# The up projection of a hybrid layer in scaled fp16 halves in place of fp32r halves

## The chip, the cores and the metric

The kernel runs on one core of one Trainium2 chip, as one launch. The metric is the device time of one execution in microseconds (us). A core has five engines that run side by side, each with a queue of its own that is worked off in order: TensorE (PE, matrix products, with its weight loads shown apart as PEld), VectorE (DVE), ScalarE (ACT), GpSimd (POOL) and SyncE (SP, which here only issues DMA transfers). They wait for one another through semaphores.

## What is computed

One layer over 1024 latent tokens of 1024 features. The change lies in the second half, the convolutional feed-forward block. Cut to what matters:

```python
def conv_ffn(h, w_up, conv_w, conv_b, w_down):
    u = h @ w_up                                  # 1024 x 1024 by 1024 x 5632
    up = jnp.pad(u, ((0, 0), (r, r), (0, 0)))     # r = 1
    acc = conv_b
    for j in range(CONV_W):                       # CONV_W = 3
        acc = acc + up[:, j:j + L] * conv_w[j]
    a, g = jnp.split(acc, 2, axis=-1)
    return (jax.nn.silu(g) * a) @ w_down
...
x = x_mid + g2 * conv_ffn(modulate(rms_norm(x_mid, norm2_w[l]), sh2, sc2), w_up[l], ...)
```

So each token is normalised, scaled and shifted channel by channel (the modulation), multiplied by the up weights, mixed with its two neighbours in every channel, gated and multiplied by the down weights.

## The kernel before, in words

**Stages.** Projections and attention come first, then the mLSTM branch, then the tail: the two branch projections and the output projection (up to about 1218 us in the profile), the up projection with convolution and gate, and the down projection (from about 1641 us). The last two share `stage_ffn` (line 2132 on); the preparation stands at the end of `stage_tail`.

**Halves.** All large products are done to nearly fp32 accuracy from two halves of each operand: `split_from` (line 50) writes `hi`, a rounded copy, on ACT (line 47, in `copy_act`), and `lo = src - hi` on DVE (line 54, or line 56, a `scalar_tensor_tensor`, where a scale is given). A product is then three matmuls, hi x hi, hi x lo and lo x hi (`product`, lines 2015 to 2017; `mm3`, lines 163 to 165). Two kinds of halves are in use. In the first stages they are fp16, with a scale from a bound on the size of the data, so that nothing overflows (`ScaledWeights`, line 90 on: ACT squares with a sum along the row, a matmul against a block of ones that adds over partitions, a power -0.5 on POOL). In the tail they are fp32r, without a scale, and each half takes as much memory as the fp32 source.

**Units.** The up projection is done in 22 units `j` of 128 columns of the first and 128 columns of the second half of the up weights. Each unit is one Strassen-like step (2 x 2 x 2 in seven products): from the weight blocks a11, a12, a21, a22 four sums s1 to s4 are made on DVE (lines 2076, 2077, 2085, 2086), and from the activations the seven operands b11, b21, t1, t2, t3, t4, b22 are made once and kept as halves for all units (`put`). In a product the halves of the weights are what PE loads, as 128x128 blocks, and the halves of the activations stream past them, 128x512 at a time; it runs over four row blocks, so it is 4 x 3 matmuls, and a unit is 84. The class `Units` holds the steps of a unit:

- `lead(j)`: the DMA of the unit's weights, 1 MB, on SP (line 2043; two buffers, pool `ffr`), and the split `r1` of a11 and a12. For unit 2 `lead_first` (line 2050) loads the half megabyte for `r1` by itself into another buffer, and `lead(2)` later the whole.
- `first_mm(j)`: products with b11 and b21. `first_ev(j)`: ACT copies bank `pa` to `ua`, DVE adds bank `pc` (line 2065).
- `prep(j)`, `prep2(j)`: the sums s1 to s4, and the splits `q1` (of s1, s2), `q2` (of s3, s4) and `r2` (of a22). `prep_apart` and `prep2_apart` do the same for unit 0 with other buffers.
- `rest(j)`: the other five products, with copies on ACT and adds on DVE (lines 2124, 2126) that empty PSUM between them.

The splits are 128x1024 values (`r1`, `q1`, `q2`) and 128x512 (`r2`); their halves lie in pools `ffo` (`op4`, ten buffers) and `ffq` (`op2`, four buffers), a buffer for each half.

After the unit's products `conv_gate` (line 2145 on) makes the three-tap convolution: ACT multiplies by the middle coefficient and adds the bias (line 2153), two `scalar_tensor_tensor` on DVE add the neighbours (2154, 2155), for both halves of the unit; ACT applies Silu to one (2158), DVE multiplies (2159), SP stores the result to `f_d` (2160). The coefficients come straight from the table `vecT`. Beside this, `sums` prepares the operands of the down projection: beside units 4 to 11 sums of down weights, later sums of the finished hidden rows (four 128x512 steps on DVE a unit, with loads and stores on SP).

**What sets the order.** The loop over `j` at the end (from line 2228 on) states the order in the source: `first_mm(j)`, `first_ev(j)`, `rest(j)`, `lead(j + 1)`, `prep(j + 1)`, `prep2(j + 1)`, `sums(j - 1)`, `conv_gate(j)`. In this part nothing is pinned by hand. The library under the kernel gives out buffers and fills each engine's queue when the program is built, from the source's order as a priority and from what is ready by then, so steps of the next unit stand in the queues among steps of this one. Once the queues are filled, each is worked off strictly.

**The start.** Before unit 0 the residual rows come out of the output projection; each block of 128 tokens gets its factor of the norm (`square`, `scale`), is transposed on PE, and leaves PSUM through `affine` (line 1878), which multiplies by `m2[:, 1]` and adds `m2[:, 0]`, the modulation. `norm_factors` computes `m2[:, 1]` once, long before.

Of the kernel before, what the change touches and what calls it, by code (L numbers as in the profile page):

```python
# [1590 lines left out]
def stage_tail(E, st):  # L1591
# [52 lines left out]

    g1b = tp1.tile([P, D], F32, name="g1b")
# [178 lines left out]
    def norm_factors():  # L1824

        nc.vector.scalar_tensor_tensor(m2[:, 1], m2[:, 1], 1.0, vecT[:, V_N2 : V_N2 + KT], op0=ALU.add, op1=ALU.mult)
        nc.vector.tensor_scalar(m2[:, 1], m2[:, 1], float(D) ** 0.5, None, op0=ALU.mult)

# [9 lines left out]
    xj = tp1.tile([P, 640], F32, name="xj")[:, :512]  # L1838
# [86 lines left out]
    def weight_sums(k, a0, a1, b0, b1, eng=None):  # L1925
# [11 lines left out]
        nc, lambda j: A["w_up"][j], lambda n: rawp.tile([P, KT, 256], F32, tag="raw", name=n), op4, op2,  # L1937
# [32 lines left out]
    scale(4)  # L1970
    U.lead(0)
    U.prep_apart(0, lambda n, dt=F32R: x512(n, dt, 1))
# [23 lines left out]
    U.lead_first(2)  # L1996
# [23 lines left out]
class Units:  # L2020
# [3 lines left out]
    def __init__(self, nc, src, raw, op4, op2, bank, out, B):  # L2024
        self.nc, self.src, self.raw, self.op4, self.op2, self.bank, self.out, self.B = nc, src, raw, op4, op2, bank, out, B
        self.raws, self.R1, self.mid, self.S, self.Q = {}, {}, {}, {}, {}
# [8 lines left out]

    def pair(self, j, nm, new, src):
        p = self.v(new(f"{nm}h{j}")), self.v(new(f"{nm}l{j}"))
        split_from(self.nc, *p, src)
        return [(p[0][:, k], p[1][:, k]) for k in range(p[0].shape[1])]

    def lead(self, j):
        self.raws[j] = raw = self.raw(f"ur{j}")
        self.nc.sync.dma_start(raw, self.src(j))
        if j != 2:
            self.R1[j] = self.pair(j, "r1", self.op4, raw[:, :, 0:P])

    def lead_first(self, j):

        raw = self.v(self.op4(f"uf{j}", F32))
        self.nc.sync.dma_start(raw, self.src(j)[:, :, 0:P])  # L2050
        self.R1[j] = self.pair(j, "r1", self.op4, raw)
# [20 lines left out]
    def prep(self, j):  # L2072
# [6 lines left out]
        self.Q[j] = [self.pair(j, "q1", self.op4, s12)]  # L2079

    def prep2(self, j):
# [5 lines left out]
        self.Q[j] += [self.pair(j, "q2", self.op4, s34), self.pair(j, "r2", self.op2, a22)]  # L2087

    def prep_apart(self, j, new):
# [3 lines left out]
        s1, s2, s3, s4 = [self.v(new(f"s{i}_{j}", F32)) for i in range(1, 5)]  # L2093
# [4 lines left out]
        self.Q[j] = [sum([self.pair(j, f"q1{i}", new, s) for i, s in enumerate((s1, s2))], [])]  # L2098
# [338 lines left out]
```

## Time and profile before

| what | value |
| --- | --- |
| time, median of 3 runs | 1852.91 us (1849.13 to 1855.06) |
| the profiled execution's own time | 1858.65 us |
| its span from first to last instruction | 1856.9 us |
| mean granted TensorE clock | 0.987 of full speed |
| up projection on PE, first to last product | 1218.75 to 1641.6 us |
| 128x512 matmuls in it | 1848 |

A row of a timeline is: start in us, duration in us, engine, line of the code, operation, `output<-inputs` by the names of the tiles, shapes and types, number of instructions, and in square brackets how long the engine had been idle before it and which instruction on which engine ended that wait. `f32` stands there for fp32r operands of matmuls, too. A row of a group ends in the total busy time and the mean duration in ns of one instruction. Matmuls overlap: the row's duration is that of one matmul from its start to its modelled end, so their rate is read from the steps between starts.

### The profile page before, as it was taken

Reading aid. Unit: us, or ns where it says so; the run is one execution under the profiler, and the core shown is the slowest. Engines: PE = TensorE matmul, PEld = TensorE weight load, DVE = VectorE, ACT = ScalarE, POOL = GpSimd, SP = SyncE. Lnnn points to the kernel's source line nnn. Section 1 sums busy time; section 2 is a strip of 40 time slices with the busy share of each in tenths; the row PEclk is TensorE's granted clock in tenths of the full one; section 3 lists DMA queues with packets and bytes.
Section 4 is the critical chain, followed back from the end, with each engine's and each line's share of the span. In section 5 each row is a group of like instructions: output and inputs, shape, how many; then the busy total and the mean of one; then the engine's idle time right before and its main releaser. Section 6 shows DMA issues by size and latency. Waiting matters only on the chain.

```text
span 1856.9 us, 27874 instructions
## 1 busy us (share of the span) xinstructions
PE 1795.2 (97%) x9207; PEld 1286.0 (69%) x9207; DVE 1418.6 (76%) x2864; ACT 1070.7 (58%) x2229; POOL 510.5 (27%) x747
## 2 busy tenths in 40 slices
PE   7889999999998899989999999999999999999999
PEld 3855555555555565656668887878888888888887
DVE  3848878888788685858687787698988998896665
ACT  4747777878787564646356563375444444464441
POOL 2467769687762630303020021000000000000000
PEclk9899999999999899999999999999999999999999
DMA  8647988888787724260449936413454544599751
GB/s 336 234 138 147 195 174 177 190 179 196 148 181 138 217 94 161 79 210 32 148 160 359 362 101 221 168 57 125 159 211 180 186 172 154 197 321 369 262 171 68
DMA packets 302193, 342.47 MB, mean 184 GB/s; under 512 B 176208, under 2 KB 200672, under 8 KB 299232
## 3 DMA queue, kind: packets, MB, share of 16 engines
q1 hardware_dynamic: 287648, 314.47, 56.1%
q10 hardware_dynamic: 14400, 26.22, 4.3%
q8 instruction: 72, 1.18, 0.3%
q14 instruction: 73, 0.60, 0.1%
HBM read 224.61 MB, written 76.16 MB: 162 GB/s over the span
## 4 chain that ended last, share of the span: by engine, by line
PE 77%; DVE 7%; DMA 5%; ACT 5%; issue 4%; POOL 3%; ACTq 0%; SPq 0%; POOLq 0%; DVEq 0%
PE g L706 8%; PE pq L706 6%; PE pa L2015 4%; PE pa L2017 4%; PE pa L2016 4%; PE po L706 3%; PE dx L2015 2%; PE dx L2017 2%; PE dx L2016 2%; PE pb L2017 2%; PE pb L2016 2%; PE pb L2015 2%; PE yb L2015 2%; PE yb L2016 2%; PE yb L2017 2%
## 5 line engine op out<-in xcount | busy, mean ns | idle before, releaser
L850 DVE CUSTOM_DVE_ANT_0 s<-s,maskA,nsink 128x640 f32<-128x640 f32 (+1 forms) x128 | 117.5, 918 | 75.0 <-PE s L845 74.6
L866 DVE TENSOR_TENSOR P<-s,P 128x640 f16<-128x640 f32 (+1 forms) x128 | 100.7, 787 | 1.0 <-ACT s L861 1.0
L860 ACT ACTIVATE P<-s,st 128x640 f16<-128x640 f32 (+1 forms) x128 | 98.3, 768 | 4.2
L706 PE MATMUL g<-hH,fh 128*128 128x512 f16 x256 | 97.9, 382 | 0.0
L706 PE MATMUL g<-hH,fl 128*128 128x512 f16 x256 | 97.8, 382 | 0.0
L706 PE MATMUL g<-hL,fh 128*128 128x512 f16 x256 | 97.7, 382 | 0.0
L861 ACT ACTIVATE s<-s,st 128x640 f32<-128x640 f32 (+1 forms) x128 | 93.9, 734 | 0.0
L706 PEld LDWEIGHTS <-hH 128*128 128x128 f16 x640 | 62.1, 98 | 36.5 <-DVE t L770 0.4
L858 ACT ACTIVATE st<-st,shift 128x1 f32<-128x1 f32 x128 | 37.6, 294 | 85.4 <-DVE st L850 84.7
L706 PE MATMUL pq<-wha,hH 128*128 128x384 f16 (+1 forms) x256 | 83.9, 328 | 0.1
L706 PE MATMUL pq<-wha,hL 128*128 128x384 f16 (+1 forms) x256 | 83.9, 328 | 0.0
L706 PE MATMUL pq<-wla,hH 128*128 128x384 f16 (+1 forms) x256 | 83.9, 328 | 0.0
L706 PEld LDWEIGHTS <-fh 128*128 128x128 f16 x512 | 48.1, 99 | 47.9 <-issue 1.6
L2153 ACT ACTIVATE cv<-ua,vecT 128x1024 f32<-128x1024 f32 x22 | 27.4, 1246 | 83.9 <-DVE ua L2126 83.9
L1424 POOL TENSOR_SCALAR kwh<-k,gcall 128x128 fp32r<-128x128 f32 x72 | 33.1, 463 | 154.4 <-PE dC L164 57.1
L163 PE MATMUL kv<-whkv,hH 128*128 128x384 f16 x192 | 63.3, 330 | 6.0 <-DVE VL L56 6.0
L2015 PE MATMUL dx<-dwh,dfh 128*128 128x512 f32 (+1 forms) x176 | 68.3, 388 | 0.0
L2017 PE MATMUL dx<-dwh,dfl 128*128 128x512 f32 (+1 forms) x176 | 68.2, 388 | 0.0
L2016 PE MATMUL dx<-dwl,dfh 128*128 128x512 f32 (+1 forms) x176 | 68.2, 387 | 0.0
L47 ACT ACTIVATE dfh<-drf 128x512 fp32r<-128x512 f32 x55 | 34.3, 628 | 58.5 <-PE dx L2016 26.0
L54 DVE TENSOR_TENSOR dfl<-drf,dfh 128x512 fp32r<-128x512 f32 x55 | 37.7, 691 | 36.5 <-ACT dfh L47 36.4
L164 PE MATMUL kv<-wlkv,hH 128*128 128x384 f16 x192 | 63.2, 329 | 0.4
(691 smaller groups left out, 6253.8 us busy)
## 6 DMA issues: line engine op xcount, KB each, us to landing
ur<-in_w_up SPq DMA_DIRECT2D x22, 1024.0 KB
wmb<-in_w_modB SPq DMA_DIRECT2D x48, 256.0 KB
f_d<-cv SPq DMA_DIRECT2D x22, 512.0 KB
wm<-in_w_modA SPq DMA_DIRECT2D x16, 512.0 KB
fr<-in_w_g SPq DMA_DIRECT2D x32, 256.0 KB
drf<-fs_d SPq DMA_DIRECT2D x15, 512.0 KB
drw<-wt_d SPq DMA_DIRECT2D x14, 512.0 KB
w1b<-in_w_cx SPq DMA_DIRECT2D x16, 388.0 KB
```

The lines of the kernel that those rows point to most:

```text
L54: rest = nc.vector.tensor_tensor(lo, src, whole, op=ALU.subtract)
L163: nc.tensor.matmul(ps, lh[:, ls], rh[:, rs], start=start and i == 0, stop=False)
L164: nc.tensor.matmul(ps, lh[:, ls], rl[:, rs], start=False, stop=False)
L706: nc.tensor.matmul(self.ps, x, w, start=self.i == 0, stop=self.i == self.n - 1)
L850: nc.vector.tensor_tensor_reduce(e, e, self.mask, scale=self.ss[:, h : h + 1], scalar=nsink[:, hh : hh + 1], op0=ALU.add, op1=ALU.min, acc ...
L858: nc.scalar.activation(m, st4[:, 8 + h : 9 + h], AF.Identity, bias=shift)
L860: nc.scalar.activation(two[:, :W], e, AF.Exp, bias=m, scale=-1.0)
L861: nc.scalar.activation(e, e, AF.Exp, bias=m, scale=-1.0, accum_out=st4[:, 4 + h : 5 + h])
L866: nc.vector.tensor_tensor(two[:, W : 2 * W], self.e[h], two[:, :W], op=ALU.subtract)
L2015: nc.tensor.matmul(ps, lh, rh, start=start and i == 0, stop=False, skip_group_check=True)
L2016: nc.tensor.matmul(ps, lh, rl, start=False, stop=False, skip_group_check=True)
L2017: nc.tensor.matmul(ps, ll, rh, start=False, stop=stop and i == n - 1, skip_group_check=True)
```

## The change

The up projection goes over to fp16 halves. Its activations are made smaller by one scale, its weights by one scale per unit, both from bounds, and the product of the two is taken off again in the coefficients of the convolution.

- `norm_factors` gets a tail: from the modulation `m2` it bounds the size of the activations (squares with sums on ACT, one matmul against the ones, a chain of tiny steps on POOL and DVE), keeps the scale and its reciprocal in `xs_` (a new 128x2 tile), and multiplies `m2` by the scale.
- `measure(j, raw)` is new, once a unit: two squares with row sums over the whole 128x2048 of raw weights on ACT, two matmuls against the ones that add up into one bank, a step on DVE that reads it, a power -0.5 on POOL (the unit's scale, `f[:, 3:4]`), its reciprocal on DVE, and on POOL the six coefficients of the convolution times both reciprocals.
- All splits of weights get the scale, so `lo` is made by line 56's form (three operands) instead of line 54's; both halves are fp16 and lie in one buffer of the same size that one fp32r half took (`pair16`, `xpair`, `pair4`, `pair2`). The splits of activations stay without a scale, with fp16 results.
- `lead` is cut in three: `fetch` (the DMA), `sizes` (`measure`) and `lead` (the split `r1`). `lead_first` goes. In the loop `fetch(j + 2)` stands ahead of `sums`, `sizes(j + 2)` after `conv_gate(j)`, and `lead(j + 1)` where it was. Before the loop, units 0 and 1 are fetched and measured ahead of their splits, and unit 2 is fetched where `lead_first` stood.
- `conv_gate` takes its coefficients from the unit's `f`.

```diff
     def norm_factors():
         nc.vector.scalar_tensor_tensor(m2[:, 1], ...)
         nc.vector.tensor_scalar(m2[:, 1], m2[:, 1], float(D) ** 0.5, None, op0=ALU.mult)
+        q = tp1.tile([P, 24], F32, name="xbound")
+        nc.gpsimd.tensor_tensor(q[:, 8:16], m2[:, 1], m2[:, 1], op=ALU.mult)
+        nc.scalar.activation(q[:, 16:24], q[:, 8:16], AF.Square, accum_out=q[:, 0:1])
+        nc.scalar.activation(q[:, 16:24], m2[:, 0], AF.Square, accum_out=q[:, 1:2])
+        pb = tp_tile("xbound")
+        nc.tensor.matmul(pb[:, 0:2], E.ones, q[:, 0:2], start=True, stop=True)
+        nc.vector.tensor_scalar(q[:, 2:4], pb[:, 0:2], 1.0, 1e-30, op0=ALU.mult, op1=ALU.add)
+        nc.gpsimd.tensor_tensor(q[:, 4:5], q[:, 2:3], expo[:, 0:1], op=ALU.pow)
...
+        nc.gpsimd.tensor_tensor(xs_[:, 0:1], q[:, 4:5], expo[:, 0:1], op=ALU.pow)
+        nc.vector.reciprocal(xs_[:, 1:2], xs_[:, 0:1])
+        nc.gpsimd.tensor_scalar(m2, m2, xs_[:, 0:1], None, op0=ALU.mult)
+
+    def measure(j, raw):
+        f = tp1.tile([P, 16], F32, tag="uf", name=f"uf{j}", bufs=4)
+        junk = xj16.rearrange("p (k c) -> p k c", k=4)
+        for i in range(2):
+            nc.scalar.activation(junk, raw[:, 4 * i : 4 * i + 4], AF.Square, accum_out=f[:, i : i + 1])
+        pb = tp_tile(f"ub{j}")
+        for i in range(2):
+            nc.tensor.matmul(pb[:, 0:1], E.ones, f[:, i : i + 1], start=i == 0, stop=i == 1)
+        nc.vector.tensor_scalar(f[:, 2:3], pb[:, 0:1], 2.0 ** -26, 1e-36, op0=ALU.mult, op1=ALU.add)
+        nc.gpsimd.tensor_tensor(f[:, 3:4], f[:, 2:3], expo[:, 0:1], op=ALU.pow)
+        nc.vector.reciprocal(f[:, 4:5], f[:, 3:4])
+        nc.gpsimd.tensor_scalar(f[:, 5:6], f[:, 4:5], xs_[:, 1:2], None, op0=ALU.mult)
+        cw = vecT[:, V_CW : V_CW + 132].rearrange("p (i u c) -> p i u c", i=3, u=2)[:, :, :, j]
+        nc.gpsimd.tensor_scalar(f[:, 6:12].rearrange("p (i u) -> p i u", i=3), cw, f[:, 5:6], None, op0=ALU.mult)
+        return f
...
     def put(m, k, src, s=slice(0, 512)):
         if B.setdefault(m, [None] * H)[k] is None:
-            B[m][k] = [x512(f"{m}{x}{k}", pool=homes[m]) for x in "hl"]
+            B[m][k] = xpair(f"{m}{k}", homes[m])
...
     scale(4)
+    U.fetch(0)
+    U.fetch(1)
+    U.sizes(0)
     U.lead(0)
-    U.prep_apart(0, lambda n, dt=F32R: x512(n, dt, 1))
+    U.sizes(1)
+    U.prep_apart(0, lambda n: x512(n, F32, 1), lambda n: xpair(n, 1))
...
     U.prep2_apart(0)
-    U.lead_first(2)
+    U.fetch(2)
...
             put("b22", k, RAW[g][k][:, cols[1]], cols[g])
+    U.sizes(2)
+    U.lead(2)
...
     def pair(self, j, nm, new, src):
-        p = self.v(new(f"{nm}h{j}")), self.v(new(f"{nm}l{j}"))
-        split_from(self.nc, *p, src)
+        p = [self.v(t) for t in new(f"{nm}{j}")]
+        split_from(self.nc, *p, src, scale=self.scale(j))
...
-    def lead(self, j):
+    def fetch(self, j):
         self.raws[j] = raw = self.raw(f"ur{j}")
         self.nc.sync.dma_start(raw, self.src(j))
-        if j != 2:
-            self.R1[j] = self.pair(j, "r1", self.op4, raw[:, :, 0:P])
-
-    def lead_first(self, j):
-
-        raw = self.v(self.op4(f"uf{j}", F32))
-        self.nc.sync.dma_start(raw, self.src(j)[:, :, 0:P])
-        self.R1[j] = self.pair(j, "r1", self.op4, raw)
+
+    def sizes(self, j):
+        self.F[j] = self.measure(j, self.raws[j])
+
+    def lead(self, j):
+        self.R1[j] = self.pair(j, "r1", self.pair4, self.raws[j][:, :, 0:P])
...
             def cw(i):
-                return vecT[:, V_CW + 44 * i + ch : V_CW + 44 * i + ch + 1]
+                o = 6 + 2 * i + (ch >= NFC)
+                return U.F[j][:, o : o + 1]
...
         if 1 <= j < NFC - 1:
-            U.lead(j + 1)
+            if j > 1:
+                U.lead(j + 1)
             U.prep(j + 1)
             U.prep2(j + 1)
...
+        if 1 <= j + 2 < NFC and j:
+            U.fetch(j + 2)
         sums(j - 1, a)
         a = conv_gate(j, *u)
+        if 1 <= j < NFC - 2:
+            U.sizes(j + 2)
```

More of the change, by code (lines that the diff above doesn't have):

```diff
@@ L2020, with __init__ @@
 class Units:
[L2024 to L2026 removed]
+    def __init__(self, nc, src, raw, op4, pair4, pair2, measure, bank, out, B):
+        self.nc, self.src, self.raw, self.op4, self.pair4, self.pair2, self.bank, self.out, self.B = nc, src, raw, op4, pair4, pair2, bank, out, B
+        self.measure = measure
+        self.raws, self.F, self.R1, self.mid, self.S, self.Q = {}, {}, {}, {}, {}, {}
     @staticmethod
```

36 lines of the change are left out of this document (26 added, 10 removed).

## The prediction

> **What bounds the kernel now.** I read the page's busy shares first, then the table of busy time by window over the up projection, then the timeline of each engine through one of its units, and last the timelines around its start.
>
> ```profile
> span 1856.9 us, 27874 instructions
> PE 1795.2 (97%) x9207; PEld 1286.0 (69%) x9207; DVE 1418.6 (76%) x2864; ACT 1070.7 (58%) x2229; POOL 510.5 (27%) x747
> 1400.00:1500.00 100.00, 100.00 (x443) 82.58 (x442) 89.54 (x107) 47.23 (x58) 0.00 (x0) 1.00 0.49 179
> ```
>
> The columns of the last row are the stretch and its length, then PE, PEld, DVE, ACT and POOL busy, the granted clock, DMA. In the middle of the up projection PE never idles, at full clock; DVE is busy 90%, ACT 47%, POOL not at all, the DMA engines half. So PE sets the pace here and DVE is second, not far behind. A busy PE may still issue slowly, so I took the step from one matmul's start to the next.
>
> ```profile
> 1300.18 0.39 PE L2015 MATMUL pa<-b11h,r1h 128*128 128x512 f32 x1
> ...
> 1312.42 0.39 PE L2015 MATMUL pb<-b22h,q2h 128*128 128x512 f32 x1
> ...
> 671.03 0.38 PE L163 MATMUL mo<-hH,wha 128*128 128x512 f16 x1
> ...
> 679.24 0.38 PE L165 MATMUL mo<-hH,wla 128*128 128x512 f16 x1
> ```
>
> The first pair spans 54 steps of the up projection without a gap: 12.24/54 = 0.2267 us. The second spans 38 steps of an earlier stage that already multiplies fp16 halves, same 128x512 shape, full clock: 8.21/38 = 0.2161 us. The change turns the first kind into the second.
>
> **Part by part. PE.** A unit issues 7 products x 4 row blocks x 3 = 84 matmuls, 22 units 1848. 1848 x (0.2267 - 0.2161) = 19.6 us less. This is a saving only where PE stays the last to be ready.
>
> The Trainium skill, "TensorE: Matmul & The Clock Gate", section "Wait — 56ns, not 53.3ns?", gives the warm step as N/2.4 + 2.5 ns, 215.7 ns at N = 512, with no term for the operands' type. The fp16 rows agree (216.1), the fp32r rows do not (226.7). By the rule this term would be nothing, and the whole change some 7 us slower; rival 3 is that case, from rows.
>
> Each `measure` puts two tiny fp32 matmuls against the block of ones into PE's queue. The nearest rows are such pairs:
>
> ```profile
> 680.10 0.28 PE L119 MATMUL wtw_ml<-wqw_ml,ones 128*128 128x4 f32 x2
> 680.24 0.36 PE L119 MATMUL wtw_mlqo<-wqw_mlqo,ones 128*128 128x4 f32 x2
> 680.46 1.74 PE L1520 MATMUL mt<-ident,hf 128*128 128x128 f32 x12
> ```
>
> One pair takes 0.14, the next 0.22 us of queue; 0.18 x 22 = 4.0 us (3.1 to 4.8), if what they multiply is there.
>
> **DVE.** Three splits of 1024 columns and one of 512 per unit become scalar_tensor_tensor; two 128x1 instructions come in.
>
> ```profile
> 1302.17 1.28 DVE L2154 SCALAR_TENSOR_TENSOR cv<-ug,vecT,cv 128x1023 f32<-128x1023 f32 x1
> 1303.37 0.69 DVE L2077 TENSOR_TENSOR s<-s,ur 128x512 f32<-128x512 f32 x1
> ...
> 1306.90 1.22 DVE L2159 TENSOR_TENSOR cv<-cv,cv 128x1024 f32<-128x1024 f32 x1
> 1308.03 0.69 DVE L2085 TENSOR_TENSOR s<-ur 128x512 f32<-128x512 f32 x1
> ...
> 1310.51 1.23 DVE L54 TENSOR_TENSOR q2l<-s,q2h 128x1024 fp32r<-128x1024 f32 x1 [0.59 <-ACT q2h L47]
> 1311.94 1.23 DVE L54 TENSOR_TENSOR r1l<-ur,r1h 128x1024 fp32r<-128x1024 f32 x1 [0.20 <-ACT r1h L47]
> ...
> 1315.12 0.69 DVE L2076 TENSOR_TENSOR s<-ur 128x512 f32<-128x512 f32 x1 [1.35 <-PE pb L2016]
> 1315.73 0.68 DVE L2126 TENSOR_TENSOR ua<-pb,ua 128x512 f32<-128x512 f32 x1
> ...
> 1334.77 0.69 DVE L2126 TENSOR_TENSOR ua<-pb,ua 128x512 f32<-128x512 f32 x1
> 1198.55 0.21 DVE L1861 TENSOR_SCALAR rrx<-rrx 128x1 f32<-128x1 f32 x1 [1.17 <-ACT xj L1858]
> L56 DVE SCALAR_TENSOR_TENSOR wlkv<-wrw_ml,wfw_ml,whkv 128x768 f16<-128x768 f32 x12 | 11.6, 1010 | 0.0
> ```
>
> Back to back the three-operand form occupies DVE 1.20 us (1302.17 to 1303.37), the two-operand form 1.13. The last row shows that an fp16 result costs nothing extra: 1.01 us at 768 columns fits 1.28 at 1023. So 4 x 0.07 = 0.28, and 2 x 0.12 for the tiny ones (a row of 0.21 whose tail overlaps the next): 0.5 us per unit. One unit is 1334.77 - 1315.73 = 19.04 us, which is 84 x 0.2267: PE's own time. In it DVE idles 0.59 and 0.20 for ACT and 1.35 for a buffer that PE still reads; the work is 19.04 - 2.14 = 16.9. The new work is 17.4, and with the two waits for ACT 18.2. PE's new unit is 84 x 0.2161 + 0.18 = 18.3. The wait for PE's buffer is slack: a pair now fits one buffer where it took two, so DVE can run further ahead. PE therefore stays the bound, by 0.1 us. That is thin, and I charge 2 us over 19 steady units for stalls that slip through (0 to the whole gain; rival 1).
>
> **ACT.** Two squares of 1024 columns with their sums per unit, and four splits with a scale from memory.
>
> ```profile
> 4.84 0.22 ACT L369 ACTIVATE sil<-vecT 128x16 f32<-128x16 f32 x1 [2.84 <-DVE vecT L367]
> 10.65 1.06 ACT L392 ACTIVATE xj<-x 128x1024 bf16<-128x1024 f32 x1 [5.60 <-DMA x<-in_ctx]
> 11.62 0.19 ACT L392 ACTIVATION_READ_ACCUMULATOR xj<-x 128x1 f32 x1
> L47 ACT ACTIVATE whkv<-wrw_ml,wfw_ml 128x768 f16<-128x768 f32 x12 | 10.5, 925 | 2.1 <-POOL wfw_ml L122 2.1
> L112 ACT ACTIVATE wjw_ml<-wrw_ml 128x768 bf16<-128x768 f32 x12 | 10.1, 842 | 9.9 <-DMA s_ba<-in_w_ba 7.2 <-DMA wrw_ml<-in_w_ml 2.1 <-ACT VH L47 0.5
> ```
>
> 2 x 1.25 for the squares; a scale from memory adds 0.08 (925 against 842 at one width), four times 0.3: 2.8 us on some 9.0 (47% of 19.04), so 12 of 18.3. The first three rows follow one another in ACT's timeline: no table is loaded between a Silu and a Square, so none is added. It costs nothing while the squares fall into ACT's waits, 4.54 and 3.11 us in one unit; with that cover gone, up to 2.8 us a unit stand before a copy that PE waits for:
>
> ```profile
> 1316.45 1.25 ACT L2153 ACTIVATE cv<-ua,vecT 128x1024 f32<-128x1024 f32 x1 [4.54 <-DVE ua L2126]
> ...
> 1318.54 0.58 ACT L47 ACTIVATE ug<-pa 128x512 f32<-128x512 f32 x1
> ...
> 1324.49 1.06 ACT L2158 ACTIVATE cv<-cv 128x1024 f32<-128x1024 f32 x1 [3.11 <-DVE cv L2155]
> ```
>
> **The added waits.** A split now waits for squares, pair, DVE, POOL's power. Behind it on ACT stand the copies that empty PSUM, for which PE waits. There are two weight buffers, so a unit's weights leave when those of two units before are read, more than a unit (18 us) ahead of their first product; the chain (2.5 + 0.2 + 0.1 + 0.6 us, the power from the row below) fits in that.
>
> ```profile
> L1862 POOL TENSOR_TENSOR rrx<-rrx,expo x8: 548/552/2466, 1180.5 to 1221.9; 128x1 f32<-128x1 f32 x8
> ```
>
> The one of 2466 ns ran while DVE was dense; even two such fit. On SP the transfer moves ahead of a unit's store of `f_d` and the loads for the next stage's sums; its buffer sets when it leaves, so passing them moves nothing, and if it did leave earlier, these 0.5 and 1 MB would come later to places that have a whole unit of time. The bound's own chain depends on `m2`, ready long before the first use, and is priced at nothing; if its cover failed, its two powers and some six tiny steps are 3 to 6 us once.
>
> **The start.** Here a step moves: unit 2 had an early half megabyte of its own; now it waits for a whole weight buffer and the chain.
>
> ```profile
> 1170.19 3.36 SPq L2043 DMA_DIRECT2D ur<-in_w_up  x2
> 1176.42 1.06 ACT L47 ACTIVATE r1h<-ur 128x1024 fp32r<-128x1024 f32 x1 [1.09 <-DMA ur<-in_w_up]
> 1220.80 0.61 SPq L2050 DMA_DIRECT2D uf<-in_w_up  x1
> 1222.40 1.23 DVE L54 TENSOR_TENSOR r1l<-ur,r1h 128x1024 fp32r<-128x1024 f32 x1
> 1238.24 0.50 PE L2015 MATMUL pa<-b11h,r1h 128*128 128x512 f32 x1 [0.22 <-ACT r1h L47]
> 1241.04 0.69 DVE L54 TENSOR_TENSOR r2l<-ur,r2h 128x512 fp32r<-128x512 f32 x1
> 1241.80 11.22 SPq L2043 DMA_DIRECT2D ur<-in_w_up  x2
> 1247.88 0.39 PE L2017 MATMUL pa<-t4h,r2l 128*128 128x512 f32 x1
> 1250.18 1.23 DVE L54 TENSOR_TENSOR q1l<-s,q1h 128x1024 fp32r<-128x1024 f32 x1
> 1252.18 0.39 PE L2015 MATMUL pa<-t2h,q1h 128*128 128x512 f32 x1
> ```
>
> Both first transfers already leave together (1170.19, two issues), so hoisting them moves nothing on SP. Unit 2's can leave when unit 0's weights are read (1241.80, right after the split at 1241.04), lands 6.2 us later (1170.19 to 1176.42) at 1248, and after chain and split serves PE at about 1253. Before, unit 2's first products filled PE in places from 1238.24 and up to 1252.18; now nothing fills there until unit 1's q1 (about 1250.2). PE's last product of unit 0 starts at 1247.88, or up to 1.4 us earlier without the six matmuls of unit 2 among them, so it idles 2.1 to 3.5 us; DVE, spared 1.1 us of unit 2's split there, may give some back. I take 2.7; the ends are 0 and 8 (unit 1 late as well). And 132 matmuls before this point (24 each in the first products of three units, 60 in the rest of one) are paced by DVE's splits of the activations, so 132 x 0.0106 = 1.4 us of the saving is not had. The half megabyte that goes frees nothing that anyone waited for.
>
> Sum: -19.6 + 4.0 + 2.0 + 2.7 + 1.4 = -9.5 us. The profiled execution took 1858.65 us, 1.75 beyond its span, and the median is 5.7 lower; 1858.65 - 9.5 = 1849.2 there, 1843.4 against the median. I say 1843.
>
> **Rivals.** 1: DVE takes over. At 17.4 of 18.3 us it has no room: if its waits for ACT grow from 0.8 to 1.4 us, a unit is 18.8 and the gain 0.24 x 20 units = 4.8 less 2.7 at the start: 1851; at 1.6 us a unit is 19.0: 1855. For it: a load of 95% in a queue that takes nothing out of turn. Against: the freed buffers, which let it work ahead.
>
> 1a, its worse end: POOL, idle until now, shuts DVE out. Three POOL steps a unit, none over the 0.55 us of the power, add at most 1.65 us: 17.4 + 0.8 + 1.65 = 19.85 a unit, 0.81 x 20 + 2.7 = 18.9 us slower, 1872. The trace shows POOL as the loser: beside the power of 2466 ns that began at 1221.9, DVE's split of 1222.40 took its usual 1.23 us. The Trainium skill, "SBUF — State Buffer", section "SBUF: two separate sides", has it that a DVE instruction with two SBUF inputs and a POOL instruction that reads SBUF exclude each other for their whole length, whoever comes first. By that rule DVE can lose too; of the two, this trace bears out only the loss on POOL's side.
>
> 2, slower: PE stalls at a pair. The pair stands in PE's queue ahead of the next unit's matmuls. If its squares were queued behind the last unit's Silu, as the source has it (1324.49 + 1.06 + 2.5 = 1328), PE, done with that unit at 1318.5 (the copy of its last bank starts at 1318.54), would wait 9.5 us. One such wait eats the gain, so it decides from there; two make 1843.4 + 19 = 1862. For it: a queue in order, and a chain over DMA, ACT, PE, DVE and POOL. Against: the queues here follow readiness and not the source. Line 2077 at 1303.37 prepares the unit after the one that PE is at, between two conv steps of the unit before it.
>
> 3: no shorter step, because 0.2267 comes from where these operands lie and not from their type: 4.0 + 2.7 = 6.7 us slower, 1860. Against it stand 38 steps in a row.
>
> **Numbers.** About 0.3% (5.6 us) is what a measurement tells from no change: 1847.3 to 1858.5. The forecast gets 0.55, with a range of its own of 1836 to 1848: the tight steady stage and the start may cost nothing (-4.7) or some 5 us more. Rival 1 gets 0.26, of which 0.05 is still faster and the rest within the bound; 1a 0.03, rival 2 0.11, rival 3 0.05, all slower. Faster 0.60, same 0.21, slower 0.19. The range 1836 to 1859 holds the forecast and rival 1 and leaves out the slower ones.
>
> **What would show it.** Step of 0.216 us between the up projection's matmuls; weight loads f16; unit to unit 18.3 to 18.5; DVE over 93% in mid-stage; squares inside ACT's waits; a PE gap of some 3 us before unit 1's q1. Wrong if units stay near 19 (rival 1), if PE idles before the pair on the ones (2), or if the step keeps 0.2267 (3).

## The result, and the profile after

The changed kernel takes 1882.92 us (median, 1880.09 to 1886.9) against 1853.99 for the kernel before on the same chip: ratio 1.016, 95% interval 1.0129 to 1.019. It is slower by 28.9 us, where 9.5 us less had been forecast.

Page and windows of the changed kernel, and then the second of these windows in the kernel before; the columns of the windows are those of the prediction's row.

```profile
span 1879.9 us, 28210 instructions
PE 1787.9 (95%) x9297; PEld 1130.3 (60%) x9297; DVE 1434.9 (76%) x2910; ACT 1124.2 (60%) x2321; POOL 571.9 (30%) x820
```

```profile
1400.00:1500.00 100.00, 94.32 (x437) 43.29 (x436) 87.26 (x111) 57.94 (x75) 11.50 (x16) 0.98 0.51 179
1500.00:1600.00 100.00, 97.79 (x463) 45.29 (x461) 92.01 (x116) 58.62 (x78) 15.98 (x15) 1.00 0.44 158
```

```profile
1500.00:1600.00 100.00, 100.00 (x443) 82.81 (x442) 86.68 (x103) 47.66 (x58) 0.00 (x0) 1.00 0.47 171
```

PE, which was busy 100 of 100 us in mid-stage, now idles, and DVE is hardly fuller than before (89.6% over the two windows, 88.1% before): nobody is saturated. PE's timeline through a unit shows that the step came out as forecast:

```profile
1574.47 0.38 PE L2066 MATMUL pa<-t,q 128*128 128x512 f16 x1 [0.44 <-ACT ua L47]
...
1582.02 0.38 PE L2068 MATMUL pa<-t,q 128*128 128x512 f16 x1
...
1587.48 0.50 PE L1863 MATMUL ub<-uf,ones 128*128 128x1 f32 x4
1587.84 0.38 PE L2066 MATMUL pa<-b,r 128*128 128x512 f16 x1
...
1593.62 0.38 PE L2066 MATMUL pa<-t,q 128*128 128x512 f16 x1 [0.44 <-ACT ua L47]
```

The first two rows are 35 steps apart: 7.55/35 = 0.2157 us, against 0.2267 before. The pair on the ones takes 0.36 us of the queue. Yet from 1574.47 to 1593.62 a unit still lasts 19.15 us, and this unit and the next begin their second group of products with a wait for ACT.

**Where the 28.9 us are.** Three marks cut the end of the kernel into parts: the last of eight `og` instructions in the output projection (ahead of all that changed but the small steps that bound the activations), the first product with `r2` in unit 0, and that in unit 21. Last `og`, before and then after (the last time in the row's range is the start of the last one):

```profile
L1846 DVE TENSOR_TENSOR og<-op,g1b x8: 683/685/692, 1134.9 to 1173.1; 128x512 f32<-128x512 f32 x8
```

```profile
L1891 DVE TENSOR_TENSOR og<-op,g1b x8: 682/684/692, 1129.1 to 1167.2; 128x512 f32<-128x512 f32 x8
```

First `r2` products of units 0 and 21, before and then after:

```profile
1244.93 0.39 PE L2015 MATMUL pa<-t4h,r2h 128*128 128x512 f32 x1
...
1638.90 0.39 PE L2015 MATMUL pa<-t4h,r2h 128*128 128x512 f32 x1
```

```profile
1255.65 0.38 PE L2066 MATMUL pa<-t,r 128*128 128x512 f16 x1
...
1661.64 0.38 PE L2066 MATMUL pa<-t,r 128*128 128x512 f16 x1
```

The *start* (from `og` to unit 0's `r2`) grew from 71.8 to 88.5 us, 16.6 more; the *units* (to unit 21's `r2`) from 394.0 to 406.0, 12.0 more; the rest to the end from 218.0 to 218.3 us. The sum is 28.9, the difference of the medians; the spans differ by less because the stages ahead ended 5.9 us earlier in the execution profiled after. All runs below are read by these two stretches.

**The start.** PE's, ACT's and SP's rows from the changed kernel's timeline:

```profile
1232.31 0.38 PE L2068 MATMUL pa<-t,q 128*128 128x512 f16 x1
...
1236.00 1.65 ACT L47 ACTIVATE t<-acc 128x512 f16<-128x512 f32 x3
1237.56 0.57 ACT L47 ACTIVATE ua<-pa 128x512 f32<-128x512 f32 x1
1238.19 0.58 PE L2066 MATMUL pa<-t,q 128*128 128x512 f16 x1 [5.50 <-ACT ua L47]
1238.57 0.63 PE L2067 MATMUL pa<-t,q 128*128 128x512 f16 x1
...
1239.95 0.33 SPq L2098 DMA_DIRECT2D ur<-in_w_up  x1
...
1241.98 0.61 PE L2066 MATMUL pa<-t,q 128*128 128x512 f16 x1
...
1244.94 1.06 ACT L1860 ACTIVATE xj<-ur 128x1024 bf16<-128x1024 f32 x1 [5.25 <-DMA ur<-in_w_up]
1246.14 0.59 PE L1863 MATMUL ub<-uf,ones 128*128 128x1 f32 x2 [3.12 <-ACT xj L1860]
```

Two things are to be seen. PE waits 5.50 us for a copy out of PSUM that stands in ACT's queue behind splits of activations (the row of 1236.00 and others ahead of it). Then unit 2's weights leave at 1239.95; ACT, with the squares next in its queue, stands still 5.25 us until they land, and PE, with the pair next in its queue, 3.12 us. After the long wait eight steps last (1241.98 - 1238.57)/8 = 0.426 us, twice the usual.

**Mid-stage.** SP's, ACT's and PE's rows between two units:

```profile
1285.55 0.33 SPq L2098 DMA_DIRECT2D ur<-in_w_up  x1
...
1293.20 1.06 ACT L1860 ACTIVATE xj<-ur 128x1024 bf16<-128x1024 f32 x1 [3.64 <-DMA ur<-in_w_up]
...
1298.04 0.58 ACT L47 ACTIVATE ua<-pa 128x512 f32<-128x512 f32 x1
...
1298.67 0.38 PE L2066 MATMUL pa<-t,q 128*128 128x512 f16 x1 [2.83 <-ACT ua L47]
```

ACT waits 3.64 us for the unit's weights before the first of its two squares; the copy `ua<-pa` comes after that square (the second square stands behind the copy), and PE waits for that copy. Nothing needs the squares yet: the pair that reads them comes in PE's queue at 1311.62. The waits from 1213 to 1665 us, of PE and then of ACT (total, times, longest):

```profile
PE pa L2066 <- ACT ua L47: 19.2, 17, 5.5
PE ub L1863 <- ACT xj L1860: 3.1, 1, 3.1
...
PE pa L2068 <- DVE r L56: 2.8, 1, 2.8
```

```profile
ACT cv L2207 <- DVE ua L2179: 54.6, 16, 5.6
ACT xj L1860 <- DMA ur<-in_w_up: 27.7, 12, 5.3
...
ACT r L47 <- POOL uf L1865: 13.2, 11, 3.5
```

So the theories: **A**, the measuring loses it, since its squares stand on ACT ahead of copies (A1: because they wait for the load; A2: by where they stand). **B**, DVE holds ACT up as soon as a unit is shorter than 19 us (B1 by its order, B2 by its amount of work). **C**, the splits wait for the chain over DVE and POOL.

### The profile page after: what moved, and what is told of

Its sections match the earlier page's. It is cut to its first block, busy times and chain, and to the rows that moved or that the text cites. A ratio compares the mean times of both kernels' runs of the same rounds, so it can differ in the third digit from the quotient of the medians.

```text
span 1879.9 us, 28210 instructions
## 1 busy us (share of the span) xinstructions
PE 1787.9 (95%) x9297; PEld 1130.3 (60%) x9297; DVE 1434.9 (76%) x2910; ACT 1124.2 (60%) x2321; POOL 571.9 (30%) x820
## 4 chain that ended last, share of the span: by engine, by line
PE 52%; DVE 20%; DMA 10%; ACT 8%; issue 5%; POOL 4%; SPq 1%; ACTq 0%; DVEq 0%; POOLq 0%
PE g L706 8%; PE pq L706 5%; PE po L706 3%; DMA ur<-in_w_up 2%; PE dx L2066 2%; PE dx L2068 2%; PE dx L2067 2%; DVE cv L2208 2%; PE dy L2066 2%; PE dy L2068 2%; PE dy L2067 2%; DVE cv L2209 2%; DVE r L56 1%; PE mo L163 1%; PE mo L164 1%
## 5 line engine op out<-in xcount | busy, mean ns | idle before, releaser
L1865 POOL TENSOR_TENSOR uf<-uf,expo 128x1 f32<-128x1 f32 x22 | 26.5, 1204 | 350.8 <-DVE uf L1864 238.2
L2066 PE MATMUL pa<-t,q 128*128 128x512 f16 x176 | 68.1, 387 | 19.2 <-ACT ua L47 19.2
L47 ACT ACTIVATE q<-s,uf 128x1024 f16<-128x1024 f32 (+1 forms) x46 | 50.7, 1106 | 41.7 <-DVE s L2139 21.0
L2067 PEld LDWEIGHTS <-q 128*128 128x128 f16 x352 | 34.7, 99 | 66.8 <-issue 29.2
```

Source lines behind the costliest of these rows:

```text
L47: return nc.scalar.activation(out, in_, AF.Copy, scale=scale)
L2066: nc.tensor.matmul(ps, lh, rh, start=start and i == 0, stop=False, skip_group_check=True)
L2067: nc.tensor.matmul(ps, lh, rl, start=False, stop=False, skip_group_check=True)
```

## The experiments

Each run's median is set against the kernel before on the same chip. "Sum" adds the changes of the two stretches against before; it agrees with the measured difference within 3.4 us, except in row 13 (5.2 us).

| run | start, us | units 0 to 21, us | sum | median | ratio, 95% interval |
| --- | --- | --- | --- | --- | --- |
| before | 71.8 | 394.0 | 0 | 1853.99 | 1 |
| after | 88.5 | 406.0 | +28.7 | 1882.92 | 1.0129 to 1.019 |
| 1 no measuring | 72.1 | 394.2 | +0.5 | 1854.59 | 0.9994 to 1.0023 |
| 2 squares of resident data | 79.6 | 406.7 | +20.5 | 1873.26 | 1.0091 to 1.0147 |
| 3 result not used | 80.6 | 400.3 | +15.1 | 1869.21 | 1.0062 to 1.0115 |
| 4 squares held | 89.5 | 399.0 | +22.7 | 1872.59 | 1.0082 to 1.0138 |
| 5 as 1, DVE relieved | 71.9 | 381.0 | -12.9 | 1840.20 | 0.9924 to 0.9962 |
| 6 as 1, rows held | 72.6 | 391.8 | -1.3 | 1850.82 | 0.9979 to 1.0011 |
| 7 as 1, sums on POOL | 78.9 | 446.0 | +59.1 | 1912.17 | 1.0308 to 1.0361 |
| 8 third raw buffer | 82.2 | 408.3 | +24.7 | 1873.62 | 1.0091 to 1.0143 |
| 9 before, DVE relieved | 73.3 | 393.9 | +1.4 | 1853.11 | 0.9996 to 1.0017 |
| 10 as 1, sums held | 72.3 | 385.1 | -8.4 | 1842.88 | 0.9935 to 0.9969 |
| 11 after, three repairs | 81.8 | 391.2 | +7.2 | 1858.12 | 1.0021 to 1.0048 |
| 12 after, DVE relieved | 88.5 | 393.4 | +16.1 | 1869.05 | 1.0078 to 1.0114 |
| 13 as 10, rows held | 72.3 | 384.5 | -9.0 | 1840.32 | 0.9892 to 0.9944 |
| 14 all a unit earlier | 82.1 | 399.8 | +16.1 | 1867.76 | 1.0043 to 1.0097 |
| 15 after, sums held | 89.2 | 400.9 | +24.3 | 1877.07 | 1.0094 to 1.0147 |
| 16 units 0 to 2 not measured | 72.6 | 400.4 | +7.2 | 1862.54 | 1.0027 to 1.0058 |
| 17 as 11, chain off DVE | 85.5 | 385.4 | +5.1 | 1857.30 | 1.0012 to 1.0035 |
| 18 as 17, unit 2's squares later | 84.6 | 386.8 | +5.7 | 1858.32 | 1.0016 to 1.0038 |

**1, no measuring.**

```diff
     def sizes(self, j):
-        self.F[j] = self.measure(j, self.raws[j])
+        pass
```

> Leaves out the measuring of the weights: every unit's halves are scaled by 512 and the convolution's 132 coefficients are made once, so no squares, no pair of ones-matmuls and no chain on GpSimd per unit; halves, products and transfers stay as in the changed kernel. Theory A (the measuring loses it: its squares stand on ACT ahead of the PSUM copies): from the last product of unit 1 to that of unit 20 the changed kernel took 368.8 us (19.41 each) and the kernel before 356.8 (18.78); this one 345 to 352 (18.2 to 18.5 each), the start of the stage is at least 10 us shorter than in the changed kernel, and the time is 1838 to 1850 us. Rival B (VectorE is the bound as soon as a unit is shorter than 19 us, with or without the measuring): still 19.0 or more a unit, 1865 to 1872 us from the shorter start alone. Rival C (only the chain's latency on GpSimd costs): as A.

The start falls back to before's; the units don't get shorter than before. The median, 1854.59, lies between the ranges of A and B. The measuring costs all 28 us, and the shorter step, without it, brings nothing: A for the loss, B for the missing gain. Its timeline in a unit, ACT's, DVE's and PE's rows:

```profile
1543.46 0.69 DVE L2228 TENSOR_TENSOR fs<-fa 128x512 f32<-128x512 f32 x1 [1.44 <-DMA fa<-f_d]
...
1545.53 0.68 DVE L2184 TENSOR_TENSOR ua<-pb,ua 128x512 f32<-128x512 f32 x1
...
1546.24 1.24 ACT L2211 ACTIVATE cv<-ua,vecT,uconst 128x1024 f32<-128x1024 f32 x1 [6.14 <-DVE ua L2184]
...
1550.91 0.57 ACT L47 ACTIVATE ua<-pa 128x512 f32<-128x512 f32 x1
...
1551.53 0.38 PE L2071 MATMUL pa<-t,q 128*128 128x512 f16 x1 [1.53 <-ACT ua L47]
```

On DVE the hidden sums (`fs<-fa`, and two more) wait for a load and stand ahead of the addition `ua<-pb`; ACT waits 6.14 us for that addition to begin a convolution; behind the convolution in ACT's queue stands the copy for which PE then waits. Two queues, each in order, hand the delay on.

**2 to 4, one part of the measuring each.** Run 2 squares a resident tile (and puts a constant in place of the sum), run 3 doesn't use the result, run 4 holds the squares:

```diff
-            nc.scalar.activation(junk, raw[:, 4 * i : 4 * i + 4], AF.Square, ...)
+            nc.scalar.activation(junk, E.there, AF.Square, ...)
...
-        return self.F[j][:, 3:4]
+        return self.uc[:, 3:4]
...
-            U.sizes(j + 2)
+            with tc.issue_after(q2_split.ins):
+                U.sizes(j + 2)
```

> The two squares of each unit read a tile of the modulated input that has long been in SBUF, not the unit's fresh weights, and the sum is multiplied by 0 and replaced by a constant, so that the scale is 512: the measuring keeps its instructions on every engine and its chain, and only the wait for the weights' transfer goes (27.7 us of ACT's idle time in 12 waits in the changed kernel). Theory A1 (ACT blocked by the transfer is what PE waits for): most of the 23 us over the kernel before in the stage's units come back, 1858 to 1868 us. Theory A2 (the 2.5 us of squares themselves, where they stand in ACT's order, hold up the copies): 1872 to 1882. Rivals B and C: no change, 1878 to 1886.

> The measuring runs as in the changed kernel, but its result is not used: splits and convolution take the constant scale 512 and coefficients made once. So the squares, the pair and the chain keep their places and their wait for the weights, and only the wait of the splits for the chain (13.2 us of ACT's idle time in 11 waits) goes. Theory A: still 1874 to 1884 us. Rival C (the splits wait for the chain on GpSimd, where the power took 1.2 us on average and up to 2.06): 1860 to 1870. Rival B: no change.

> Only the order on ACT changes: from unit 3 on, a unit's two squares are held behind the split of the second sums (q2) of the unit ahead of it, at a time when its weights landed most of a unit ago and ACT then waits about 3 us for the rest of the unit (before the first convolution step). Theory A: no more waits of the squares for the transfer from unit 3 on, 18.4 to 18.8 us a unit, so 11 to 19 us less than the changed kernel: 1864 to 1872 us; the start keeps its loss. Rival B (VectorE): 19.1 or more a unit, 1876 or more. Rival C: the chain now starts later, so the splits wait longer and the time is not below 1880.

Run 2: without the wait for the load 8.9 us come back, all of it at the start; in the units, where most of the 27.7 us of ACT's waits lay, taking them away changes nothing in sum (406.7), so A1 is wrong there. Its total fits A2. But the queues were filled anew for this run: in most units of mid-stage both squares now stand right ahead of the copy `ua<-pa`, and the splits' wait for the chain grew from 13.2 to 31.8 us. So it doesn't show that the waits by themselves were free. Run 3: using the result costs 5.7 us in the units and 7.9 at the start; C is real, which A had denied (1874 or more). Run 4: the squares' place costs 7.0 us in the units; the median is just above what A gave, and the units, 19.0 us on average, are longer than its 18.4 to 18.8.

**5 and 9, DVE relieved.** Three of the four sum subtractions go, in run 5 from run 1's kernel and in run 9 from the kernel before, so that the down projection gets partly wrong operands:

```diff
         sub(a0, a1, a0)
-        sub(a1, b1, a1)
-        sub(b1, b1, a0)
-        sub(b0, b0, b1)
+        if k < 3:
+            ...
```

> On the kernel without measuring (1854.6 us; 18.8 us a unit where TensorE alone would need 18.1): of the four subtractions per unit that make the down projection's sums, three are left out (the sums of weights from the fourth pair on, and of hidden blocks; what is stored is partly the data as loaded, and hidden sums take one buffer fewer), so VectorE has 1.8 us less per unit, and loads and stores stay. Theory B (with the shorter step VectorE's in-order queue, 15.8 to 17.6 us of work in 18.8, is what PE's copies wait for in the end): 18.1 to 18.4 us a unit and 1841 to 1848 us. Rival D (the copies on ACT are late by themselves, VectorE has nothing to do with it): 1852 to 1857.

> The kernel before (fp32r halves, 19.04 us a unit) with the same three of four sum subtractions left out as in the run that fell to 18.13 us a unit. Theory B says that before the change TensorE was the bound and VectorE had room: still 19.04 us a unit and 1849 to 1855 us, so that all of the step's gain shows only when VectorE is relieved as well. If the time falls by more than 4 us, the relief itself and not the step made that run fast.

Run 5: units of 18.13 us, 84 steps and nothing else, from unit 7 on; the median, 1840.20, is just below what B gave. Run 9: still 19.04. So the kernel before is bound by PE and has room on DVE; with the short step DVE's room is gone. 18.13 against 19.04 is the step's whole gain, and in these runs it comes only with DVE relieved; run 10 below tells whether it is the work or its order.

**7, the weights' sums on POOL.**

```diff
+        t = self.nc.gpsimd.tensor_tensor
         t(s12[:, 0:4], a21, a22, op=ALU.add)
```

> On the kernel without measuring: the four sums of weight blocks per unit (s1 to s4, 0.6 us each on VectorE) are made by GpSimd, which is idle in that kernel's up stage, from unit 1 on. Theory B: VectorE has 2.4 us less per unit; if GpSimd takes 1.5 us or less for each, 18.1 to 18.5 us a unit and 1840 to 1849 us. If GpSimd is held off beside a dense VectorE as the power was in the changed kernel (1.2 us on average, 2.06 at most, for one element a partition), its four operations and the splits behind them come late: 1857 or more. Rival D: 1852 to 1857.

The groups of this kernel, and then the same DVE instruction of run 1 (mean ns in the middle):

```profile
L2136 POOL TENSOR_TENSOR s<-s,ur 128x512 f32<-128x512 f32 x19 | 39.1, 2059 | 1.5
L2145 POOL TENSOR_TENSOR s<-ur 128x512 f32<-128x512 f32 x19 | 27.8, 1463 | 166.4 <-PE pb L2073 142.9 <-DVE wa L1939 11.2 <-DVE fs L2230 11.1
```

```profile
L2214 DVE SCALAR_TENSOR_TENSOR cv<-ug,uconst,cv 128x1023 f32<-128x1023 f32 x19 | 37.4, 1966 | 0.0
```

```profile
L2212 DVE SCALAR_TENSOR_TENSOR cv<-ug,uconst,cv 128x1023 f32<-128x1023 f32 x20 | 25.5, 1277 | 0.0
```

POOL takes 1.46 to 2.06 us where DVE took 0.6, and this instruction of DVE grows from 1.28 to 1.97 us: each holds the other off. The Trainium skill, "SBUF — State Buffer", section "SBUF: two separate sides", has a DVE instruction with two SBUF inputs and a POOL instruction that reads SBUF exclude each other for a whole instruction, whoever comes first; this run agrees with that, for both sides.

**10, 13, 15, the sums held; 6, the rows held.**

```diff
+        with tc.issue_after(U.ua_add.ins):
             sums(j - 1, a)
...
+            with tc.issue_after(E.fd.ins), tc.issue_after(E.cv.ins):
                 last_row()
```

> On the kernel without measuring, with all its work: the four sum subtractions of a unit are held on VectorE behind the last addition out of PSUM of the unit's second half (ua<-pb), which stood behind them and for which ACT then waited up to 6.1 us. Theory B1 (the order on VectorE makes the waits): 18.2 to 18.6 us a unit and 1843 to 1850 us. B2 (it is the amount: 15.8 to 17.6 us of work in a unit of 18.1, in any order): 1852 to 1857.

> On the kernel without measuring: the last 16 rows of the modulation product (load and one VectorE operation of 0.75 us each), nine of which run during units 0 to 6 in it and ran behind the up stage in the kernel before, are held behind the last convolution step and the last store of the up stage. Theory B: VectorE has 6.8 us less to do in the windows where it is 97 per cent busy (135.2 of 140 us from 1260 to 1400), and behind the stage it has room: 1848 to 1852 us. Rival D: 1853 to 1857; if the rows are then late for the end of the kernel, more.

> On the kernel without measuring and with the sum subtractions held (1842.9 us; 18.13 us a unit from the twelfth, but 21.1 and 22.0 in units 5 and 6): the sixteen modulation rows are held behind the up stage as well. If the nine rows that run in units 0 to 6 are what fills VectorE there, these two units fall to 18.1 to 19 and the time to 1836 to 1840 us; if the stall there is of the sums' own (their loads, which first come in unit 4), 1841 to 1845.

> The changed kernel, all work and the measuring in its place, with only the sum subtractions held behind the last addition out of PSUM on VectorE. If the order on VectorE is at the root of the late copies (B1): 10 us or more come back, 1866 to 1873. If the squares' place on ACT holds the copies up whatever VectorE does (A2): under 6 us, 1877 to 1884.

Run 10 has all of DVE's work of run 1 and only another order. From 1375 us to 1640 this is all that PE waits for, and DVE is fuller than in the windows above (third busy time):

```profile
PE pa L2071 <- ACT ua L47: 0.3, 1, 0.3
```

```profile
1400.00:1500.00 100.00, 99.59 (x461) 44.95 (x460) 94.59 (x113) 52.39 (x62) 0.00 (x0) 1.00 0.54 192
```

So B1, from 1375 us on: the order, not the amount. Units 5 and 6, ahead of that, stay long. Run 6 shortens the units by 2.4 us, but its interval and that of run 1 overlap. Run 13 brings units 5 and 6 from 21.14 and 22.00 us to 19.13 and 18.80, but unit 8 then takes 22.08 (DVE waits 1.59 us for a load of down weights there), and the stretch gains 0.6 us; the median lies between the two ranges, and the rows are at most part of it. Run 15: with the measuring in place, the sums' order is worth 5.1 us in the units, less than B1 wanted and what A2 gave.

**12, the measuring with DVE relieved.** Edit as in run 5, on the changed kernel.

> The changed kernel with its measuring, and three of the four sum subtractions left out (1.8 us less on VectorE per unit). If the measuring costs its 28 us by its own place on ACT (A): the relief brings no more than it did without measuring (14 us), 1865 to 1872. If it costs them because VectorE is too full to make up for any delay (B): more than that, 1845 to 1860, and units of 18.5 us (84 steps and the pair of ones-matmuls).

The relief brings 12.6 us in the units, 13.2 without measuring: in sum the two costs are separate (A). But most late units last 18.49 us, 84 steps and the pair, which had been B's sign: there the squares, in the place that they have in the changed kernel, cost PE nothing.

**8 and 16, the start.** A third raw buffer; and constant scales for units 0 to 2.

```diff
-    rawp, op4p, op2p = left("ffr", 2), left("ffo", 10), left("ffq", 4)
+    rawp, op4p, op2p = left("ffr", 3), left("ffo", 8), left("ffq", 4)
...
+        if j < 3:
+            nc.gpsimd.memset(f[:, 3:4], 512.0)
+            ...
+            return f
```

> The changed kernel with its measuring, and a third buffer for the raw weights (paid for by two of the ten buffers for splits): unit 2's load no longer waits for unit 0's last split, and later loads leave a unit earlier, so no squares meet a load that has not landed. Theory A1 at the start (the transfer of unit 2's weights, issued at 1239.95, holds ACT for 5.25 us and PE with it): unit 0's last product starts at about 1245 in place of 1255.7 and 1868 to 1874 us; between units 1 and 20 little changes, as with the resident data (368.5 against 368.8 us). Rival (the start loses by the order of the squares and splits, not by the transfer): 1878 or more.

> The changed kernel, with the first three units' scale a constant (512): no squares, pair or chain for units 0 to 2, and from unit 3 on all as in the changed kernel. If the start's loss (unit 0's last product 10.7 us later than before the change) is the measuring of these three units: it starts at 1243 to 1246 and the time is 1867 to 1873 us. If it is the load of unit 2 that waits for a whole buffer and the order around it: 1878 or more.

Run 8 takes 6.3 us off the start (and adds 2.3 to the units), run 16 15.9 of the 16.6 (its total is below what was expected, since the units gain 5.6 as well): the start's loss is the measuring of three units, and 6 (run 8) to 9 us (run 2) of it is the late load.

**11, 14, 17, 18, repairs together.** Run 17's chain:

```diff
-        nc.vector.tensor_scalar(f[:, 2:3], pb[:, 0:1], 2.0 ** -26, 1e-36, ...)
+        copy_act(nc, f[:, 2:3], pb[:, 0:1], 2.0 ** -26)
...
-        nc.vector.reciprocal(f[:, 4:5], f[:, 3:4])
+        nc.gpsimd.tensor_tensor(f[:, 4:5], f[:, 2:3], f[:, 3:4], op=ALU.mult)
```

> The changed kernel, all work and the measuring kept, with three repairs at once: squares held behind the q2 split (1872.6 us alone), a third raw buffer (1873.6 alone) and the sum subtractions held behind the last addition out of PSUM. If what they mend is separate: about 10 us for the order of the squares, 9 for the start and 4 to 8 for the sums, so 1855 to 1862 us. If they mend the same waits twice, or VectorE's amount of work is the limit (B2): 1866 to 1873.

> All work and the measuring kept. The three repairs together (1858.1 us), the rows held behind the stage, and each unit's load, squares and chain one unit earlier, which the third raw buffer allows. In the three repairs' kernel the split of r still waited 57.6 us in 19 waits for the chain (VectorE's small operation came 5 us after the squares, and the power took 1.5 us), in units of 18.9 us. If that wait is the rest of the measuring's cost: 18.5 us a unit (84 steps and the pair of ones-matmuls) and 1846 to 1852 us. If not: 1855 to 1859.

> All work and the measuring kept, the three repairs of the 1858.1 us kernel (18.9 us a unit) and the rows held behind the stage; the chain behind the pair leaves VectorE's queue (the factor 2^-26 is put on by ACT, the reciprocal is a product on GpSimd), where its first small operation ran 5 us after the pair; and the splits of r and the second sums are held behind the copy of the unit's first product. If the splits' wait for the chain is the rest of the measuring's cost: 18.5 us a unit and 1848 to 1853 us. If the squares' 2.5 us on ACT cost by themselves: 18.9 a unit still and 1856 to 1860.

> The run before in this list, with unit 2's squares also held behind the last split of b22, since they stood at 1223.7 to 1226 among the activations and splits for which TensorE waits at the start. If the start's rest of loss is ACT's load there: 2 to 5 us less than that run. If unit 2's halves then come late: the same or more.

Run 11 lands where separate repairs add up. Run 14 missed: with the loads a unit earlier the queue's builder drew the splits forward too (the split `r1` stands 31.4 us ahead of the unit's first product, 11.8 in run 11, medians of units 6 to 19), they waited as long as ever for the chain (63.0 us), and units grew to 19.55. Run 17 takes two of DVE's small steps out of the chain; beyond run 11 it also holds the rows, and the splits `r1`, `q2` and `r2` behind the copy `ua<-pa`. In the units these together do what was hoped; which of them did it wasn't tested. PE's waits from 1303 to 1636 us, and two units:

```profile
PE pa L2066 <- ACT ua L47: 0.7, 1, 0.7
```

```profile
1543.49 0.38 PE L2066 MATMUL pa<-t,r 128*128 128x512 f16 x1
...
1561.98 0.38 PE L2066 MATMUL pa<-t,r 128*128 128x512 f16 x1
```

18.49 us: the squares are hidden wholly, and the pair is what is left of the measuring. The kernel still takes 0.12 to 0.35% more than before (1857.30 us, not 1848 to 1853), by a start of 85.5 us against 71.8; run 18's one move there didn't shorten it measurably. A version that does all the work and beats the kernel before was not found; runs 10 and 13, which beat it, leave the measuring out.

## Why the prediction was wrong

By stretches: the sum had +2.7 for the start and -19.6 + 4.0 + 2.0 + 1.4 = -12.2 for the units. They came out at +16.6 and +12.0. Of the 24.2 us that the units miss, 16.4 are there without any measuring (run 1) and 7.8 come with it.

- **PE's step** (-19.6): right, 0.2157 us measured; where nothing else holds PE, a unit is 18.13 us. That alone decides rival 3 (no).
- **The pair** (+4.0): 0.36 us, not 0.18; 7.9 for 22. The two rows taken as two pairs are one matmul each. The count shows it: 22 units have 44 such matmuls, and the changed kernel has 88 records of them, two for each. So the two rows together, 0.36 us from 680.10 to 680.46, were the price of one pair.

```profile
L1863 PE MATMUL ub<-uf,ones x88: 164/250/373, 1201.0 to 1626.0; 128*128 128x1 f32 x88
```

- **DVE** (+2.0): the largest failure. "PE therefore stays the bound, by 0.1 us. That is thin, and I charge 2 us" was a comparison of amounts. Run 1 has the whole gain gone (394.2), 16.4 us more than the -16.2 that the sum gives without the pairs; that is rival 1, in the form in which a unit stays near 19 us. But not because DVE was full: run 10 has DVE busy 94.6%, and from 1375 us on PE waits once, 0.3 us. The step that failed is that slack was counted in busy time, when what runs out first is the order: an addition that ACT needs stands on DVE behind sums that nobody needs yet.
- **ACT's squares** (0) and **the added waits** (0): "It costs nothing while the squares fall into ACT's waits" and "the chain (...) fits in that" both took the queue to have the squares when it had time for them. They stand far ahead of need, in front of copies in a queue that keeps its order. Their place costs 7.0 us in the units (run 4), the wait for the chain 5.7 (run 3). The chain had been given 3.4 us (2.5 + 0.2 + 0.1 + 0.6). In the changed kernel it lasts 22.3 us from a unit's first square to the end of its power (median of units 6 to 19), and 13.1 of them pass between the end of the squares and the pair, which stands late in PE's queue. The unit's split `r1` on ACT starts 0 to 1.9 us after the power ends, and that is still some 15 us ahead of the unit's first product: the splits, too, stand early. One unit, in the changed kernel:

```profile
1492.70 1.06 ACT L1860 ACTIVATE xj<-ur 128x1024 bf16<-128x1024 f32 x1 [5.17 <-DMA ur<-in_w_up]
1498.63 1.05 ACT L1860 ACTIVATE xj<-ur 128x1024 bf16<-128x1024 f32 x1
...
1512.23 0.50 PE L1863 MATMUL ub<-uf,ones 128*128 128x1 f32 x4
...
1514.33 1.52 POOL L1865 TENSOR_TENSOR uf<-uf,expo 128x1 f32<-128x1 f32 x1 [19.81 <-ACT ug L47]
1516.87 1.75 ACT L47 ACTIVATE r<-ur,uf 128x1024 f16<-128x1024 f32 x2
```

  Together with the sums' order (5.1, run 15) the three come to 17.8 of the 20.6 us between the changed kernel's units and run 17's; that they add up so was not shown, since run 17 changes more than these.
- **The start** (+2.7): right in what is late (unit 2's whole buffer), wrong in who waits. The sum had PE out of work for 3 us. PE's five longest waits there are 13.4 us (0.8 in all before), and sixteen half-speed steps after two of them cost some 3.4: about the 16.6. Of the waits, 3.12 are for the squares that wait for the load, 5.50 for a copy that stands behind splits on ACT, and the rest for splits of weights on ACT and DVE. The bound of 8 was too low; run 16 shows that it is the measuring.
- **Rivals.** 1 happened, for the gain. 2 (PE at the pair) happened once, 3.12 us. No rival's time reaches 1883 (the latest is 1872), since none gives ACT's squares and the splits' wait a price. 1a: beside the tiny steps DVE wasn't seen to lose; with real work on POOL (run 7) both did. The `m2` chain and SP's move cost nothing that shows.

What stays open: which of ACT's instructions at the start must move to win back the remaining 13 us of run 17, why the pair stands so late in PE's queue, and why the hole of units 5 and 6 moves to unit 8.

## What to carry to other kernels

A step that lets PE run 5% faster brought nothing here until the engines that empty its banks had an instruction order that keeps up. Ask not how busy the second engine is, but what stands in its queue ahead of the one instruction that the bound waits for. Work with no deadline (sums, squares) belongs behind an instruction that has one, by an explicit edge: one edge was worth 9.1 us here (run 10 against run 1). Before a new chain is priced at nothing because it has time, look where each queue, filled from expected readiness, will put its part of the chain: here one matmul pair stood 13.1 us behind its input.

## What the runs showed of the hardware that had not been expected

- fp32r operands cost 0.2267 us a step, fp16 ones 0.2157, at 128x512 and full clock.
- After PE's 5.50 us wait, steps took 0.426 us for some 4 us. The Trainium skill, "TensorE: Matmul & The Clock Gate", section "Part 1: The HAM clock gate (the "warmup" mystery)", gives half the clock after an idle window of about 3.4 us. The trace agrees on the half: the granted clock is 0.50 from 1235.61 to 1242.43 us. On the length it differs: after the wait of 3.12 us the clock is 0.50 again (1245.85 to 1249.26), though PE had worked 0.59 us in the 3.42 us before. In run 17 this follows a wait of 2.84 us (0.50 from 1224.80 to 1228.21); the same wait in the changed kernel (up to 1223.88) was not followed by it. A stall at PE can therefore cost more than its length.
- POOL's power on one element a partition took 0.55 us alone (the prediction's row) and 1.2 on average beside the units' DVE work, by its group in the changed kernel:

```profile
L1865 POOL TENSOR_TENSOR uf<-uf,expo 128x1 f32<-128x1 f32 x22 | 26.5, 1204 | 350.8 <-DVE uf L1864 238.2
```
